# The softmax over a sequence's pages, traced in four parts between the next sequence's page steps

## The chip, the cores and the metric

The kernel runs on one core of a Trainium2 chip. It is one inference step of a one-layer hybrid decoder: a prompt of 1024 tokens and a sample group of 8 sequences, each with one new token and 4096 past ones. The metric is the device time of one execution in microseconds (us). The core has five engines that work side by side, each through its own instructions in order: TensorE (PE) for matrix products, VectorE (DVE), ScalarE (ACT), GpSimd (POOL), and SyncE (SP), which here mostly starts DMA transfers.

## The reference

One projection of the normalised input feeds three groups of heads: differential attention, a Mamba-2 SSD scan and a gated delta rule (GDN). Their outputs are joined, projected and added to the input. For the change only the attention of the sample group matters. Its keys and values lie in pages of 128 tokens, 32 for each sequence, found by a page table:

```python
k_past = cache_k[l, page_table].reshape(bs, past, H_A, 2 * DH_A)
v_past = cache_v[l, page_table].reshape(bs, past, H_A, DV_A)
...
logits = jnp.einsum('bqhmd,bkhmd->bmhqk', q, k).astype(jnp.float32) * (DH_A ** -0.5)
logits = logits + rel_pos_bias(q_pos, k_pos, table)
...
p = jax.nn.softmax(logits, axis=-1)
wts = p[:, 0] - lam * p[:, 1]
return jnp.einsum('bhqk,bkhd->bqhd', wts.astype(v.dtype), v)
```

There are 4 heads with two maps each, so 8 softmaxes for each sequence, over its 4096 past keys and its own new one; the weights are the first map's less lambda times the second's.

## The kernel before, in words

**Streams.** The work is written as Python generators. Each does a piece of work and then yields a number, the amount of it. `drive()` (L280) always advances the generator whose done share of its total is least, so the yielded numbers set how the pieces are interleaved in the program. The order in the program is in its turn the priority by which a scheduler orders each engine's instructions. The projection stream (`proj_fm`, L424, matmuls in L458) is the longest; it fills TensorE between 107 and about 870 us, beside the GDN stream (on VectorE the steps of a triangular solve, tile `U`, through the helper in L159) and the sample stream. In the last stretch the prompt's attention (scores L718 and L719, values L745), the rest of GDN, the SSD scan (L1268 to L1329), the single-token steps and the rest of the sample stream are interleaved.

**The sample stream** (`sample_attention`, L903) takes the sequences one after the other. For sequence b there are 16 page steps (`k_pages`, L835): SyncE starts the transfers of two pages of keys (L823), GpSimd multiplies them by the query (L840), and VectorE sums the products (L841) into the scores `lg`. Between the page steps of sequence b the values of sequence b - 1 are used: `v_load` (L883) takes one of three buffers `vt`, of two pages each, and `v_mul` (L889) multiplies two such buffers, four pages, with the weights `wz` into the one PSUM bank `pv` (L896). A `v_mul` is eight instructions on TensorE, and its first waits for all four pages. Below, such four pages are a group, numbered 0 to 7 in each sequence; sequences are numbered from 0.

**The softmax** (`page_softmax`, L843) follows when all pages of keys of b have been summed: the largest score on each partition (VectorE, `smx`), a transposition on TensorE (L851), the largest over the partitions and a diagonal matrix (VectorE, `sm` and `sdg`), a product that gives it to all partitions (L856), the subtraction (VectorE, after the copy `spm`), the exponential (ScalarE, `lg` and `ses`), sums (VectorE, `ssm`), a product that adds them over the partitions (L868), and on VectorE the division and the weights `wz` and `wself`. GpSimd clears the columns of `wz` that the sequence before used (L875). In the program all of this is one piece that yields 4.0.

SyncE also starts the loads and stores of other streams, in the same queue as the pages: the stores of the attention's output (`oA` to `mixd`, L531) and of the scan's (`yv` to `mixd`, L1329), and loads of Y (L1268), of GDN states (`gs`) and of the output projection's weights (`wo`, L1552).

Of the kernel before, what the change touches and what calls it, by code (L numbers as in the profile page):

```python
# [23 lines left out]
NS = 8  # L24
# [54 lines left out]
def bl(ap, n):  # L79
    return ap.unsqueeze(len(ap.shape)).broadcast_to(list(ap.shape) + [n])  # L80


def bm(ap, n):
    return ap.unsqueeze(1).broadcast_to([ap.shape[0], n] + list(ap.shape[1:]))
# [3 lines left out]
def trunk_kernel(  # L88
# [43 lines left out]
    def nm(s):  # L132
        uid[0] += 1
        return f"{s}_{uid[0]}"
# [4 lines left out]
    def half(shape=(P, 512), dt=F32, n="h"):  # L139
        return hp.tile(list(shape), dt, tag="h", name=nm(n))  # L140
# [4 lines left out]
    def bank(ring=None):  # L145

        r = ring or rings[-1]
        return PS[r].tile([P, 512], F32, tag="b", name=nm("b"))

    def small(shape, n, dt=F32, bufs=2):  # L150
        return sp.tile(shape, dt, tag=n, name=nm(n), bufs=bufs)

    def act(out, in_, func, bias=0.0, scale=1.0, accum=None):
        if accum is None:
            return S.activation(out, in_, func, bias=bias, scale=scale)  # L155
        return S.activation(out, in_, func, bias=bias, scale=scale, accum_out=accum)  # L156

    def tt(out, a, b, op):
        return V.tensor_tensor(out=out, in0=a, in1=b, op=op)  # L159
# [675 lines left out]
    def k_pages(b, qb, lg, g):  # L835
        kt = kvp.tile([P, 2, 512], F32, tag="kt", name=nm("kt"), bufs=KB)
        for j in range(2):
            page(cache_k, b * NPG + 2 * g + j, kt[:, j, :])
        with behind_gdn():
            G.tensor_tensor(out=kt, in0=kt, in1=bm(qb, 2), op=ALU.mult)  # L840
            V.tensor_reduce(out=lg[:, 2 * g:2 * g + 2, :], in_=kt.rearrange("p j (a d) -> p j a d", d=64), axis=AX.X, op=ALU.add)  # L841

    def page_softmax(b, lg):  # L843
        l31 = lg[:, NPG - 1, :].rearrange("p (h m) -> p h m", m=2)
        tt(l31, l31, bl(fb, 2), ALU.add)
        mx = small([P, 8], "smx")
        V.tensor_reduce(out=mx, in_=lg.rearrange("p g a -> p a g"), axis=AX.X, op=ALU.max)
        tt(mx, mx, slfb[:, b, :], ALU.max)

        pt = bank()  # L850
        TE.transpose(pt[0:8, 0:P], mx, ident)  # L851
        m8 = small([8, 1], "sm8")
        V.tensor_reduce(out=m8, in_=pt[0:8, 0:P], axis=AX.X, op=ALU.max)
        dg = small([8, 8], "sdg")
        V.tensor_scalar_mul(dg, ident[0:8, 0:8], m8)
        TE.matmul(pt[:, 256:264], ones[0:8, :], dg, start=True, stop=True)  # L856
        pmx = small([P, 8], "spm")
        V.tensor_copy(pmx, pt[:, 256:264])
        tt(lg, lg, bm(pmx, NPG), ALU.subtract)
        act(lg, lg, AF.Exp)  # L860
        es = small([P, 8], "ses")
        tt(es, slfb[:, b, :], pmx, ALU.subtract)
        act(es, es, AF.Exp)
        sm = small([P, 8], "ssm")
        V.tensor_reduce(out=sm, in_=lg.rearrange("p g a -> p a g"), axis=AX.X, op=ALU.add)
        tot = small([P, 8], "sto")
        pt = bank()
        TE.matmul(pt[:, 0:8], ones, sm, start=True, stop=True)  # L868
        tt(tot, pt[:, 0:8], es, ALU.add)
        V.reciprocal(tot, tot)  # L870
        tt(tot, tot, lsg.rearrange("p h m -> p (h m)"), ALU.mult)
        tt(lg, lg, bm(tot, NPG), ALU.mult)
        l4 = lg.rearrange("p g (h m) -> p g h m", m=2)
        if b > 0:
            G.memset(wz[:, :, 4 * b - 4:4 * b], 0.0)  # L875
        tt(wz[:, :, 4 * b:4 * b + 4], l4[:, :, :, 0], l4[:, :, :, 1], ALU.add)
        tt(es, es, tot, ALU.mult)
        e2 = es.rearrange("p (h m) -> p h m", m=2)
        tt(wself[:, b, :], e2[:, :, 0], e2[:, :, 1], ALU.add)

    vq = []

    def v_load(b, g):  # L883
        vt = kvp.tile([P, 2, 512], F32, tag="vt", name=nm("vt"), bufs=VB)
        for j in range(2):
            page(cache_v, b * NPG + 2 * g + j, vt[:, j, :])
        vq.append((b, g, vt, pages[-2:]))
# [13 lines left out]
                mybir.DependencyClass.Sync, mybir.DependencyReason.DATA), reason="four pages at once")  # L901

    def sample_attention():  # L903
        for b in range(NS + 1):
            if b < NS:
                qb = half(n="qb")
                SP.dma_start(out=qb, in_=qd[b:b + 1, :].broadcast_to([P, 512]))
                lg = small([P, NPG, 8], "lg")
            vg = 0
            for g in range(NPG // 2):  # L910
                if b < NS:
                    k_pages(b, qb, lg, g)
                    yield 2.4
                if b > 0:
                    want = 16 if b == NS else max(0, g - 2) * 16 // 13 + 1
                    while vg < min(16, g + VB if b == NS else want + 1):
                        if len(vq) == VB:
                            v_mul()
                            yield 1.0
                        v_load(b - 1, vg)  # L920
                        vg += 1
                    while len(vq) > 1 and vg - len(vq) + 1 < want and g > 2:
                        v_mul()
                        yield 1.0
            while vq:
                v_mul()
                yield 1.0
            if b < NS:
                page_softmax(b, lg)
                yield 4.0  # L930
        wd = small([NS, NS, 4], "wd", bufs=1)
        tt(wd, wself[0:NS], bl(ident[0:NS, 0:NS], 4), ALU.mult)
        TE.matmul(pv[0:32, :], wd, vS, start=False, stop=True)
        hm = small([P, 4], "hm", bufs=1)
        V.tensor_reduce(out=hm, in_=ident.rearrange("p (a h) -> p h a", h=4), axis=AX.X, op=ALU.add)
        sb = small([P, NS], "sb", bufs=1)
        V.tensor_reduce(out=sb, in_=ident.rearrange("p (j b h) -> p b j h", b=NS, h=4), axis=AX.XY, op=ALU.add)
        pvs = half(n="pvs")
        tt(pvs.rearrange("p (h d) -> p h d", d=P), pv.rearrange("p (h d) -> p h d", d=P), bl(hm, P), ALU.mult)
        pst = bank()  # L940
        TE.matmul(pst[0:NS, :], sb, pvs, start=True, stop=True)
        oS = half([NS, 512], n="oS")
        S.copy(oS, pst[0:NS, :])
        finish_sample(oS, 0)
        yield 1.0
# [733 lines left out]

    sample_q()  # L1680
    smp = sample_attention()
    drive((chain(items(1), small_cols()), 52.0), (take(smp, 16 * 2.4 - 0.1), 40.0))
    sample_k()
# [251 lines left out]
```

## Time and profile before

| | |
|---|---|
| time, median of 3 runs | 1310.28 us (1307.37 to 1313.32) |
| profiled execution | 1304.49 us |
| its span from first to last instruction | 1302.8 us |
| TensorE busy, matmuls | 1156.6 us, 89% |
| VectorE busy | 855.5 us, 66% |
| GpSimd busy | 585.1 us, 45% |
| ScalarE busy | 464.0 us, 36% |
| data moved by DMA | 275.56 MB, 212 GB/s in the mean |

The span is what the rows of the trace cover; the execution's own time is some 2 us longer. A row of the trace that names a wait (in square brackets, behind "idle before") tells how long the engine stood idle just ahead of the instruction and what then released it. An engine that is busy for less than the whole span need not be a limit, and its idle time costs nothing unless something that the end depends on is behind it.

### The profile page before, as it was taken

The page shows a single profiled execution, that of the slowest core. Times are in us where ns is not written, and L with a number is a line of the kernel's source. Part 1 is how long each engine was busy: PE and PEld are TensorE (multiplying, and loading weights), DVE is VectorE, ACT ScalarE, POOL GpSimd, SP SyncE. Part 2 cuts the span into 40 slices and gives each one's busy share as a digit, 9 for nine tenths or more (in the row PEclk, how much of TensorE's full clock was granted, in tenths as well). Part 3 has the DMA queues.
Part 4 walks back from the last instruction along what each step waited for, and adds up shares of the span by engine and source line. Part 5 has one row for each costly group of instructions (what it writes and reads, how often), then busy time and mean ns, then how long its engine had stood idle before and what let it go on. Part 6 is the DMA issues. An engine that isn't in the chain of part 4 may idle for free.

```text
span 1302.8 us, 22109 instructions
## 1 busy us (share of the span) xinstructions
PE 1156.6 (89%) x7445; PEld 970.2 (74%) x7445; DVE 855.5 (66%) x1994; ACT 464.0 (36%) x991; POOL 585.1 (45%) x395
## 2 busy tenths in 40 slices
PE   4999999979899989888987997878788899799997
PEld 3889897857688778768867786765566778688876
DVE  6624495398477769557449725878759879674444
ACT  6332232212223312324522242334527658552111
POOL 3757873463545653556546655633012232151100
PEclk9999998989899889999889998979889989899999
DMA  8656864985876953985876889799587373871410
GB/s 294 192 183 213 286 208 154 301 285 170 290 237 213 305 177 113 287 278 167 292 222 211 254 282 270 229 286 257 143 243 198 103 182 109 293 237 49 145 67 34
DMA packets 246450, 275.56 MB, mean 212 GB/s; under 512 B 31905, under 2 KB 163376, under 8 KB 246322
## 3 DMA queue, kind: packets, MB, share of 16 engines
q1 hardware_dynamic: 168082, 214.44, 52.1%
q10 hardware_dynamic: 78256, 59.72, 16.1%
q8 instruction: 59, 0.97, 0.3%
q14 instruction: 53, 0.43, 0.1%
HBM read 231.59 MB, written 42.67 MB: 211 GB/s over the span
## 4 chain that ended last, share of the span: by engine, by line
PE 44%; DMA 22%; DVE 19%; issue 4%; SPq 4%; POOL 3%; ACT 3%; ACTq 1%; POOLq 0%; DVEq 0%
PE b L458 16%; PE b L1824 9%; DMA kt<-in_cache_k_dram 4%; DMA vt<-in_cache_v_dram 4%; DVE U L159 4%; PE pv L896 4%; DVE lg L841 3%; DVE cy L167 2%; POOL kt L840 2%; DMA ql<-qfd 1%; DMA w<-in_w_in_dram 1%; SPq L823 1%; PE b L745 1%; DMA sbc<-bcd 1%; PE b L1051 1%
## 5 line engine op out<-in xcount | busy, mean ns | idle before, releaser
L458 PE MATMUL b<-hh,whi 128*128 128x344 f32 (+1 forms) x2016 | 505.2, 333 | 5.9 <-ACT whi L155 2.4
L840 POOL TENSOR_TENSOR kt<-kt,qb 128x1024 f32<-128x1024 f32 x128 | 307.0, 2403 | 228.0 <-DMA kt<-in_cache_k_dram 160.2
L458 PEld LDWEIGHTS b<-hh,whi 128*128 128x128 f32 x2016 | 358.9, 194 | 39.0 <-issue 28.1
L458 PE MATMUL b<-hh,wlo 128*128 128x344 f32 (+1 forms) x1008 | 330.2, 332 | 3.1 <-POOL wlo L201 2.9
L841 DVE TENSOR_REDUCE lg<-kt 128x16 f32<-128x1024 f32 x128 | 155.2, 1214 | 133.4 <-POOL kt L840 126.3
L458 PEld LDWEIGHTS b<-hh,wlo 128*128 128x128 f32 x1008 | 195.1, 194 | 20.8 <-issue 16.5
L201 POOL TENSOR_TENSOR wlo<-w,whi 128x512 fp32r<-128x512 f32 x86 | 111.6, 1302 | 99.9 <-ACT whi L155 87.2
L1824 PE MATMUL b<-wo,mh 128*128 128x512 f32 (+1 forms) x408 | 122.0, 381 | 0.3 <-POOL wo L1558 0.3
L896 PE MATMUL pv<-vt,wz 128*32 128x512 f32 x512 | 82.6, 671 | 23.5 <-DMA vt<-in_cache_v_dram 16.0
L155 ACT ACTIVATE whi<-w 128x512 fp32r<-128x512 f32 x86 | 53.9, 629 | 134.4 <-PE b L458 89.1
L167 DVE SCALAR_TENSOR_TENSOR cy<-b,vec,cy 128x341 f32<-128x341 f32 (+4 forms) x180 | 99.7, 566 | 1.6
L1824 PEld LDWEIGHTS b<-wo,mh 128*128 128x128 f32 x408 | 75.0, 189 | 14.9 <-POOL wo L1558 0.5
L1824 PE MATMUL b<-wo,ml 128*128 128x512 f32 (+1 forms) x204 | 77.2, 379 | 0.0
L1792 POOL TENSOR_TENSOR ml<-zt,mh 128x512 fp32r<-128x512 f32 x16 | 22.5, 1406 | 106.3 <-ACT mh L1791 101.3
L159 DVE TENSOR_TENSOR U<-U,Dm 128x60 f32<-128x60 f32 (+24 forms) x124 | 51.4, 415 | 24.9 <-DMA Dm<-invd 23.1
L156 ACT ACTIVATE e<-e,nmx 128x128 f32<-128x128 f32 (+7 forms) x64 | 49.0, 768 | 13.2 <-DVE nmx L723 7.0
L155 ACT ACT_TABLE_LOAD x30 | 38.5, 1283 | 40.0 <-DMA w<-in_w_in_dram 15.8
L718 PE MATMUL b<-kTh,qh 128*128 128x128 f32 (+3 forms) x96 | 41.8, 437 | 8.8 <-DVE mx L721 8.5
L159 DVE TENSOR_TENSOR y<-b,gate 128x512 f32<-128x512 f32 (+1 forms) x17 | 11.1, 660 | 52.4 <-PE b L1824 52.4
L159 DVE TENSOR_TENSOR U<-U 128x60 f32<-128x60 f32 (+24 forms) x124 | 44.0, 355 | 1.8
L969 DVE TENSOR_SCALAR cy<-b,vec 128x344 f32<-128x344 f32 (+1 forms) x60 | 33.4, 565 | 15.9 <-PE b L458 15.8
L1824 PEld LDWEIGHTS b<-wo,ml 128*128 128x128 f32 x204 | 38.4, 188 | 7.1
(528 smaller groups left out, 2032.3 us busy)
## 6 DMA issues: line engine op xcount, KB each, us to landing
kt<-in_cache_k_dram SPq DMA_DIRECT2D x256, 256.0 KB
vt<-in_cache_v_dram SPq DMA_DIRECT2D x256, 256.0 KB
w<-in_w_in_dram ACTq DMA_DIRECT2D x82, 256.0 KB
zfd<-zf ACTq DMA_DIRECT2D x12, 512.0 KB
wo<-in_w_out_dram SPq DMA_DIRECT2D x12, 512.0 KB
om<-mixd SPq DMA_DIRECT2D x24, 256.0 KB
xt<-in_x_prompt_dram SPq DMA_DIRECT2D x8, 512.0 KB
hx<-in_w_ada_dram SPq DMA_DIRECT2D x16, 256.0 KB
```

The costliest lines, as they stand in the source:

```text
L155: return S.activation(out, in_, func, bias=bias, scale=scale)
L156: return S.activation(out, in_, func, bias=bias, scale=scale, accum_out=accum)
L159: return V.tensor_tensor(out=out, in0=a, in1=b, op=op)
L167: return V.scalar_tensor_tensor(out=out, in0=a, scalar=s, in1=b, op0=op0, op1=op1)
L201: G.tensor_tensor(out=lo, in0=w32, in1=hi.bitcast(F32), op=ALU.subtract)
L458: TE.matmul(ps[:, 0:N], a, b[k][:, sl], start=(i == 0), stop=(i == 23))
L718: TE.matmul(ps[:, 0:b - a], qh[:, m, ts], kT[m][:, a:b], start=True, stop=False)
L840: G.tensor_tensor(out=kt, in0=kt, in1=bm(qb, 2), op=ALU.mult)
L841: V.tensor_reduce(out=lg[:, 2 * g:2 * g + 2, :], in_=kt.rearrange("p j (a d) -> p j a d", d=64), axis=AX.X, op=ALU.add)
L896: mm = TE.matmul(pv[32 * r:32 * r + 32, :], wz[:, 2 * g + j, :], vt[:, j, :], start=(b == 0 and g < 2), stop=(b == NS - 1 and g >= 14 and ...
L969: V.tensor_scalar_mul(y[:, c0_:c0_ + m], ps[:, o:o + m], wv[3])
L1824: TE.matmul(ps[c], m[a][:, kt % 4, :], w[kt][:, c[0]:c[1]], start=(kt == KT[0] and i == 0), stop=(kt == KT[-1] and i == 2))
```

## The change

`page_softmax` becomes a generator with four parts. The first ends after the largest score on each partition, the second after the diagonal matrix, the third after the sums, and the fourth is the rest. The second product (L856, 859 after) takes a PSUM bank of its own instead of the transposition's. In `sample_attention` only the first part is traced right behind a sequence's page steps; the other three come one at a time behind the first three page steps of the next sequence, each with a yield of 1.3. For the last sequence, which has no next one, they come one after the other ahead of the page loop, each with a yield of 4.0.

```diff
@@ page_softmax
         V.tensor_reduce(out=mx, in_=lg.rearrange("p g a -> p a g"), axis=AX.X, op=ALU.max)
         tt(mx, mx, slfb[:, b, :], ALU.max)
+        yield
 
         pt = bank()
         TE.transpose(pt[0:8, 0:P], mx, ident)
...
         V.tensor_scalar_mul(dg, ident[0:8, 0:8], m8)
+        yield
+        pt = bank()
         TE.matmul(pt[:, 256:264], ones[0:8, :], dg, start=True, stop=True)
...
         tot = small([P, 8], "sto")
+        yield
         pt = bank()
         TE.matmul(pt[:, 0:8], ones, sm, start=True, stop=True)
...
         tt(wself[:, b, :], e2[:, :, 0], e2[:, :, 1], ALU.add)
+        yield
@@ sample_attention
     def sample_attention():
+        soft = None
         for b in range(NS + 1):
...
             vg = 0
+            if b == NS:
+                for _ in soft:
+                    yield 4.0
             for g in range(NPG // 2):
                 if b < NS:
                     k_pages(b, qb, lg, g)
                     yield 2.4
+                if soft is not None and next(soft, 0) is None:
+                    yield 1.3
                 if b > 0:
...
             if b < NS:
-                page_softmax(b, lg)
-                yield 4.0
+                soft = page_softmax(b, lg)
+                next(soft)
```

Lines below the softmax have other numbers after: the products L896 are L901, and the scan's L1268 and L1329 are L1279 and L1340. The engines run the same instructions in another order. Three places show it. The first is TensorE's order at the end of sequence 4's values, before; `vt` is a buffer of two pages, `b` a PSUM bank of the projection, `hh` and `wlo` or `whi` its operands.

```order
L458 MATMUL b_7353<-hh_773,wlo_7088 128x344
L896 MATMUL pv<-vt_7283,wz 32x512 x2
L896 MATMUL pv<-vt_7343,wz 32x512 x2
L896 MATMUL pv<-vt_7383,wz 32x512 x2
L896 MATMUL pv<-vt_7460,wz 32x512 x2
L458 MATMUL b_7425<-hh_514,whi_7253 128x344
```

And after, at the same place:

```order
L901 MATMUL pv<-vt_7230,wz 32x512 x2
L901 MATMUL pv<-vt_7318,wz 32x512 x2
L458 MATMUL b_7438<-hh_514,whi_7277 128x344
L458 MATMUL b_7438<-hh_515,whi_7277 128x344
...
L458 MATMUL b_7572<-hh_515,whi_7277 128x344
L901 MATMUL pv<-vt_7356,wz 32x512 x2
L901 MATMUL pv<-vt_7422,wz 32x512 x2
```

Group 7 followed group 6 with nothing between; now 50 matmuls of the projection stand between the two.

The second place is TensorE's order at the end of the last sequence's values, sequence 7, after; `kTh` and `qh` are operands of the prompt's scores.

```order
L901 MATMUL pv<-vt_10907,wz 32x512 x2
L901 MATMUL pv<-vt_10919,wz 32x512 x2
L718 MATMUL b_11455<-kTh_10514,qh_11218 128x512
L719 MATMUL b_11455<-kTh_10514,ql_11219 128x512
L718 MATMUL b_11461<-kTh_10517,qh_11218 128x256
L719 MATMUL b_11461<-kTh_10517,ql_11219 128x256
L901 MATMUL pv<-vt_10966,wz 32x512 x2
L901 MATMUL pv<-vt_10978,wz 32x512 x2
L944 MATMUL pv<-vS,wd_11061 32x512
```

Four matmuls stand between groups 6 and 7 here. Before, the same two groups had 46 rows between them, among them these, which led up to the last group:

```order
L745 MATMUL b_10391<-vh_9746,wT_10367 128x128
L1291 LDWEIGHTS identb
L1291 MATMUL b_10783<-masks,identb 128x512
L1293 MATMUL b_10783<-nsels,rts 128x512
L1296 MATMUL b_10783<-rts,sels 128x128 x4
L1492 MATMUL b_10434<-gs_11122,gwz_11124 32x128 x8
L745 MATMUL b_10503<-vh_9746,wT_10452 128x128 x2
L896 MATMUL pv<-vt_10761,wz 32x512 x2
L896 MATMUL pv<-vt_10773,wz 32x512 x2
L933 MATMUL pv<-vS,wd_10808 32x512
```

The other streams' rows that stood there now stand elsewhere.

The third place is SyncE's queue among the last sequence's pages of values, after; an ISA row ahead of a page computes its address.

```order
L823 DMA vt_10721<-in_cache_v_dram 128x512
L531 DMA mixd<-oA_9481 128x8x128
L1340 DMA mixd<-yv_10066 128x512
L823 ISA
L823 DMA vt_10733<-in_cache_v_dram 128x512
L823 ISA
L823 DMA vt_10733<-in_cache_v_dram 128x512
L814 TENSOR_LOAD pt_1086
L823 ISA
L823 DMA vt_10749<-in_cache_v_dram 128x512
```

Before, the first store of `oA` stood behind the last page:

```order
L823 DMA vt_10773<-in_cache_v_dram 128x512
L1520 DMA gs_11566<-in_state_gdn_dram 128x8x128
L1520 DMA gs_11718<-in_state_gdn_dram 128x8x128
L531 DMA mixd<-oA_9444 128x8x128
L1329 DMA mixd<-yv_10068 128x512
```

So two stores of other streams now stand ahead of pages of sequence 7 that stood ahead of them.

## Rows read from the trace of the kernel before

**Rows 1.** The page: busy time of the engines; shares of the chain that ended last.

```profile
PE 1156.6 (89%) x7445; PEld 970.2 (74%) x7445; DVE 855.5 (66%) x1994; ACT 464.0 (36%) x991; POOL 585.1 (45%) x395
PE 44%; DMA 22%; DVE 19%; issue 4%; SPq 4%; POOL 3%; ACT 3%; ACTq 1%; POOLq 0%; DVEq 0%
```

**Rows 2.** TensorE's waits: line, releaser: us in total, times, longest us.

```profile
PE pv L896 <- DMA vt<-in_cache_v_dram: 16.0, 10, 4.6
PE b L851 <- DVE smx L159: 12.3, 4, 9.0
...
PE b L868 <- DVE ssm L865: 8.5, 3, 4.3
...
PE b L868 <- DVE U L159: 6.5, 1, 6.5
...
PE pv L896 <- DVE wz L159: 4.2, 3, 2.0
...
PE pv L896 <- DMA kt<-in_cache_k_dram: 2.8, 1, 2.8
```

**Rows 3.** TensorE's timeline, 452 to 464: start, us, line, tiles, count, [idle before].

```profile
453.17 1.06 PE L896 MATMUL pv<-vt,wz 128*32 128x512 f32 x8 [0.89 <-DMA vt<-in_cache_v_dram]
...
460.64 1.94 PE L896 MATMUL pv<-vt,wz 128*32 128x512 f32 x8 [4.56 <-DMA vt<-in_cache_v_dram]
```

**Rows 4.** TensorE's timeline, 673 to 683.

```profile
673.38 0.48 PE L458 MATMUL b<-hh,whi 128*128 128x344 f32 x2
673.70 0.32 PE L458 MATMUL b<-hh,wlo 128*128 128x344 f32 x1
673.95 1.06 PE L896 MATMUL pv<-vt,wz 128*32 128x512 f32 x8
679.39 1.94 PE L896 MATMUL pv<-vt,wz 128*32 128x512 f32 x8 [4.37 <-DMA vt<-in_cache_v_dram]
...
682.28 0.78 PE L458 MATMUL b<-hh,whi 128*128 128x344 f32 x2
```

**Rows 5.** TensorE's timeline, in 345 to 365 and in 638 to 641.

```profile
349.97 1.21 PE L896 MATMUL pv<-vt,wz 128*32 128x512 f32 x8 [2.84 <-DMA kt<-in_cache_k_dram]
...
639.38 1.07 PE L896 MATMUL pv<-vt,wz 128*32 128x512 f32 x8 [1.50 <-DMA vt<-in_cache_v_dram]
```

**Rows 6.** TensorE's timeline, 898 to 990.

```profile
949.71 1.94 PE L896 MATMUL pv<-vt,wz 128*32 128x512 f32 x8 [0.62 <-DMA vt<-in_cache_v_dram]
...
955.57 1.06 PE L896 MATMUL pv<-vt,wz 128*32 128x512 f32 x8 [0.41 <-DMA vt<-in_cache_v_dram]
956.56 0.50 PE L718 MATMUL b<-kTh,qh 128*128 128x512 f32 x1
956.90 0.39 PE L719 MATMUL b<-kTh,ql 128*128 128x512 f32 x1
```

**Rows 7.** TensorE's timeline, 857 to 868.

```profile
858.48 1.07 PE L896 MATMUL pv<-vt,wz 128*32 128x512 f32 x8
...
865.75 1.57 PE L896 MATMUL pv<-vt,wz 128*32 128x512 f32 x8
```

**Rows 8.** Timeline of all engines, 279 to 291.5.

```profile
282.61 2.34 POOL L840 TENSOR_TENSOR kt<-kt,qb 128x1024 f32<-128x1024 f32 x1
282.78 2.26 DVE L159 TENSOR_TENSOR U<-U,Dm 128x68 f32<-128x68 f32 x1
...
290.67 0.37 PE L851 MATMUL b<-ident,smx 128*8 128x128 f32 x1 [9.02 <-DVE smx L159]
```

**Rows 9.** A window: width; busy us of PE, PEld, DVE, ACT, POOL.

```profile
925.00:950.00 25.00, 18.40 (x115) 12.43 (x119) 21.91 (x117) 14.28 (x43) 1.04 (x1) 0.77 0.54 165
```

**Rows 10.** Instructions of the tile `ses`: durations in ns, min/median/max.

```profile
L159 DVE TENSOR_TENSOR ses<-slfb,spm x8: 153/160/2357, 195.4 to 918.2; 128x8 f32<-128x8 f32 x8
```

**Rows 11.** SyncE's waits: line, releaser: us in total, times, longest us.

```profile
SPq L531 <- DVE oA L159: 23.5, 4, 12.3
SPq L1268 <- PE b L1314: 16.9, 5, 8.3
```

## Prediction, made before the changed kernel was run

> **What bounds the kernel now.** I read the page's busy line and the shares of its chain first. TensorE is busy for 1156.6 of 1302.8 us, VectorE 855.5, GpSimd 585.1; the chain that ended last is TensorE for 44%, DMA 22%, VectorE 19% [rows 1]. TensorE works in order, so the span is its work plus its waits, and a change that removes no arithmetic can only move the waits. Then the list of TensorE's waits [rows 2], for what the softmax and the page products touch. The products `pv` wait for pages of V 16.0 us in 10 places, and 2.8 us in one that is put down to a page of K. The softmax makes it wait at the transposition L851 (12.3 us in 4, the longest 9.0), at the sum L868 (8.5 us in 3, the longest 4.3, and one of 6.5 behind a step of U), and at the first product of a sequence for `wz` (4.2 in 3). These add to 50.3 us, 4% of the span: the whole field of this change.
>
> Then the timelines about the longest of them. One `pv` row is eight instructions, four pages, and waits for all four. Three buffers of two pages are turned over, so two pages of a group can be fetched only when the group ahead is done. In [rows 3] a group starts at 453.17, lasts 1.06, and the next starts at 460.64 after a wait of 4.56: 6.4 us from an end to the next start is what two late pages take. In [rows 4] it is 675.01 to 679.39, 4.4 us, with nothing at all between. Before the wait one matmul of the projection takes 0.32 us and two take 0.48, so each further one costs 0.16; just behind it two take 0.78: the granted clock has fallen towards its lower level. So 6.4 us holds 40 such matmuls, and two groups that are closer stand still for the rest.
>
> **The change part by part.** No instruction's arithmetic goes or comes, and one bank more is taken for each softmax; the parts and their `yield`s are no instructions. The sum goes against the profiled execution, 1304.5 us, 5.8 below the median of the runs, 1310.3.
>
> *Waits for pages that go.* The softmax's weight in the interleaving is now spread over three steps, and so the groups of `pv` stand elsewhere among the projection's matmuls. In TensorE's order of before, the distance of a group from the one ahead, its own four rows counted, is 4 to 22 rows in seven places, and 37 to 54 after: sequence 1's group 4 (22 to 41), sequence 2's groups 6 and 7 (20 to 41, 12 to 47), sequence 4's groups 3 and 7 (14 to 37, 4 to 54), sequence 7's groups 3 and 4 (13 to 43, 15 to 39). Their waits: 2.84 [rows 5], 0.89 and 4.56 [rows 3], 4.37 [rows 4], 0.62 and 0.41 [rows 6]; and 1.50 for sequence 4's group 3 [rows 5]. Sum -15.2. The 3.6 us that are left of the 18.8 stand at places whose distances hardly change.
>
> *Waits for pages that come.* Other pairs move together. Sequence 6's groups 4 and 5 go from 40 and 29 rows to 24 and 25. In [rows 7] the 25 rows between its groups 4 and 5 of before were 29 less the group's own four; they took from 859.55 to 865.75, 6.2 us, 0.25 each. The 20 and 21 rows that stay are then 5.0 and 5.2 us: short by 1.4 and 1.2. Sequence 7's group 6 goes from 28 to 22 rows: 18 at 0.25 is 4.5, short by 1.9. Its group 7 goes from 50 to 8: four score matmuls remain, the like of which start 0.2 to 0.3 us apart [rows 6], so 1.0 us of 6.4 is covered, short by 5.4. Sequence 1's group 6 goes from 37 to 10 rows, but TensorE's few rows there stand in the delta rule's chain, which waits for VectorE and ScalarE of itself; I take 0.5, near the end of nothing, for the group ahead waited there too [rows 5] (0 to 5.4 are the ends). Sum +10.4 (5, where only the last pair isn't hidden, to 15).
>
> *The softmax's own waits.* The longest transposition wait, 9.02 us [rows 8], is that of sequence 1. It stays: TensorE's order has this transposition at the same place as before, since only page steps, which put nothing on TensorE, were put ahead of it. At the sum L868: sequence 7's 4.29 goes, since 88 instead of 19 matmuls now stand between L856 and L868 (-4.3; nothing if VectorE, busy for 21.9 of 25 us there [rows 9], is late with whatever takes its place). Sequence 5's wait of 6.5 behind U [rows 2] has 16 matmuls more ahead (2.6 us) and two VectorE rows more (0.43 us each, 855.5 over 1994): -1.7. Sequence 6's 1.7, part of the 8.5, has three matmuls more and seven VectorE rows more: +2.5. At the first product of the next stage, waiting for `wz`, the matmuls between L868 and it go from 71, 59, 55, 37, 37 to 45, 39, 46, 38, 31 for sequences 1 to 5, with VectorE rows 24, 20, 27, 14, 22 to 22, 19, 22, 15, 23. Three of these are the waits of [rows 2] (4.2 us), those of sequences 3 to 5; sequences 1 and 2 had none and lose 26 and 20 matmuls of their slack, which no row gives. By 0.16 and 0.43 us a row I take -0.7, +0.3 and +1.4 for the three, and, between nothing and the 4.2 and 3.2 us of those matmuls, +1.0 and +1.4 for the first two. All together about 0 (-6 to +10).
>
> *Cost at nothing.* The further bank: its first use is in the ring of banks that the softmax already drew from twice, and the transposition's bank is now free earlier; no wait of [rows 2] is for a bank of these. The clear of `wz` on GpSimd for sequence 7 now stands behind the last multiply of keys, so that multiply no longer waits with it; VectorE, not that multiply, is late there.
>
> *A rule weighed.* The softmax's steps of VectorE now stand among the page multiplies of GpSimd. What the trace shows: a step of U beside a multiply of 2.34 us took 2.26 [rows 8], and the small subtraction `ses`, 160 ns in the median, took 2357 ns once [rows 10]. The Trainium skill, "SBUF — State Buffer", section "Who interferes with whom", says that a VectorE instruction with two SBUF inputs and a GpSimd instruction that reads SBUF exclude each other for a whole instruction; these rows agree. By that rule every two-input step of parts two to four risks a multiply's length. By the rows the risk is not new: multiplies ran on both sides of the softmax already, and the extreme of 2357 is from before the change. I put nothing into the sum, and a rival below.
>
> The sum: 1304.5 - 15.2 + 10.4 + 0 = 1299.7 for a profiled execution, and with 5.8 more 1305 as a median.
>
> **The rivals.** Bound of telling: 0.5%, 6.5 us; within it a measurement of this kernel can't tell a change.
>
> *Waits go and nothing takes their place.* If the new close pairs are hidden (TensorE waits for something else between them, as the 0.25 us a row of [rows 7], more than the 0.16 of the projection alone, says that it did) and VectorE keeps up, it is -15.2 - 4.3 - 1.7, some -21, with the clock's recovery behind each wait (0.15 us for each of a few matmuls) on top; half of the new pairs hidden gives -15. Time 1289 to 1300, the middle 1295. For it: the seven places were much too close before, and the new ones mostly nearly fit. Against it: the last pair with 8 rows can't be hidden by its neighbours.
>
> *The last V pages stand behind a store.* The slower side. SyncE issues in order. Before, the store of head 0's output (L531) stood behind the last page of sequence 7. In the new order of SyncE the stores of the attention output (L531) and of `yv`, and a load of Y (L1268, 1279 after), stand between pages of sequence 7. SyncE's waits there are up to 12.3 and 8.3 us [rows 11]; both would hold pages back by up to 20.6 us, and a `pv` that lacks a page holds all that is behind it on TensorE. Less the 6.4 that one group's turn-over covers, that is 14: 1305 + 14 = 1319. It decides when TensorE reaches a group of sequence 7 before its store's data are there. Against it: the products of this sequence were moved back by some 40 to 180 rows too, and so more of the head's work is done by then.
>
> *Stretched softmax.* If the two two-input steps between L856 and L868 are each caught by a multiply, a softmax is later by twice the 2.2 us of [rows 10]; for seven, half of it uncovered, 15 us: 1320. For it: nothing keeps the multiplies away. Against it: the two steps had multiplies beside them before.
>
> *The change does next to nothing*, because its parts mostly keep their place on TensorE, as the 9.02 us wait does: 1308 to 1312. It falls into the forecast's own band.
>
> **How the numbers follow.** The forecast's case with the last rival beside it, within 0.5% of 1310.3: 0.40. Waits go: 0.38, faster. The store: 0.17, stretched softmax: 0.05, both slower. The forecast is 1305, near the edge of "faster", since a sum of terms of both signs gave -5; all its bounds at one end or the other (-15.2 with +5 and -6, or with +15 and +10) are 1294 and 1320, and half-way to each, its own range, 1300 to 1312. The whole range reaches from 1287 (all waits gone, and the clock) to 1324 (the store's price in full).
>
> **What would show it.** In the changed profile: the wait of `pv` for pages in the list falls from 18.8 to about 14 us, with the longest single one in sequence 7's last group, about 5; the 9 us transposition wait is still there; at L868 it waits about 4.8 and 4.3 us for sequences 5 and 6, and not for 7. It is wrong if `pv` waits in sequence 7 are above 10 us, if SyncE's L531 row has a page of V next to it, or if waits not named here (L718, L1216, L1291) grow by more than the sum.

## The result, and the profile after

The changed kernel is slower: 1323.77 us in the median of 8 runs (1316.21 to 1329.48), beside 1311.6 us for the kernel before (8 runs, 1305.91 to 1313.96). The ratio is 1.0096, with a 95% interval of 1.0068 to 1.0124; the forecast was 1305 us and "within 0.5%". The ratios here and below leave disturbed runs out, so they can differ a little from the quotient of two medians.

The profiled execution of the changed kernel has a span of 1323.9 us, 21.1 more than the one before; it is among the slower ones, so its sizes are larger than the median's 12. First the page: busy times of the engines, as in [rows 1], and the granted clock in 40 slices.

```profile
PE 1174.1 (89%) x7442; PEld 981.8 (74%) x7445; DVE 872.0 (66%) x1994; ACT 472.1 (36%) x996; POOL 584.8 (44%) x395
...
PEclk9999999989999999988888999967798899899999
```

TensorE does the same instructions and is busy 17.5 us longer. It runs longer at the lower clock: the slices with 6 and 7 are those between 860 and 960 us. The mean granted clock over all runs says the same: 0.9346 (8 runs), and 0.9394 for the kernel before (118 runs, from all comparisons). A run's time multiplied by its mean clock is roughly what it would take at full clock: 1236.4 us (standard error 1.7) after and 1229.3 (0.5) before. So of the 14 us between the two means some 7 are waiting and 7 are the lower clock; this is an estimate, since it lets waits shrink with the clock too. In the profiled pair the clock's part is larger: of the 21.1 us, 17.5 are longer busy time of TensorE and 3.6 more idle time.

Where is the time lost? The projection's last matmul (L458) starts at 860.8 us before and 862.0 after; the output projection's first starts at 1142.1 and 1163.2. Nearly all 21 us lie between the two, in the last stretch. There the table by windows says what happened; the columns are as in [rows 9], and the last three are granted clock, DMA share and GB/s. Before:

```profile
860.00:890.00 30.00, 21.92 (x120) 15.85 (x119) 24.92 (x79) 16.89 (x38) 10.52 (x6) 0.72 1.02 292
...
930.00:960.00 30.00, 25.71 (x149) 16.08 (x147) 23.27 (x126) 13.65 (x39) 1.73 (x4) 0.81 0.69 205
960.00:1000.00 40.00, 36.42 (x268) 28.70 (x267) 26.96 (x65) 20.35 (x61) 14.14 (x19) 1.00 0.84 229
1000.00:1040.00 40.00, 34.53 (x320) 29.61 (x318) 33.32 (x101) 28.55 (x79) 7.28 (x5) 1.00 0.44 120
```

And after:

```profile
860.00:890.00 30.00, 16.07 (x75) 10.04 (x75) 23.19 (x65) 11.04 (x25) 10.96 (x6) 0.60 0.97 250
...
930.00:960.00 30.00, 24.20 (x127) 19.85 (x128) 23.55 (x124) 20.59 (x63) 1.96 (x4) 0.73 0.20 63
960.00:1000.00 40.00, 38.06 (x253) 30.20 (x251) 32.59 (x98) 17.73 (x52) 15.03 (x19) 0.88 0.96 249
1000.00:1040.00 40.00, 33.40 (x270) 21.04 (x267) 19.87 (x72) 23.25 (x66) 3.79 (x3) 0.89 0.63 184
```

Three things are to be seen. Just behind the projection's end TensorE does 75 matmuls where it did 120. From 930 to 960 the DMA share is 0.20 where it was 0.69: the loads of V stand still, since their buffers are full and the products that would empty them can't run; the next load leaves at 967.2 us, just behind the first of these products. And from 960 on, where the clock was at its full level before, it is 0.88 and 0.89.

The reason for the second is the last softmax. Its chain before, on VectorE and TensorE (start, us, line, tiles; `smx` to L851, `sdg` to L856, `ssm` to L868):

```profile
912.46 0.42 PE L851 MATMUL b<-ident,smx 128*8 128x128 f32 x1
915.01 0.21 DVE L855 TENSOR_SCALAR sdg<-ident,sm 8x8 f32<-8x8 f32 x1
916.12 0.38 PE L856 MATMUL b<-sdg,ones 8*128 8x8 f32 x2
927.07 0.60 DVE L865 TENSOR_REDUCE ssm<-lg 128x8 f32<-128x256 f32 x1
927.73 0.59 PE L868 MATMUL b<-ssm,ones 128*128 128x8 f32 x2 [4.29 <-DVE ssm L865]
```

After:

```profile
918.44 0.41 PE L852 MATMUL b<-ident,smx 128*8 128x128 f32 x1
919.20 0.22 DVE L856 TENSOR_SCALAR sdg<-ident,sm 8x8 f32<-8x8 f32 x1
933.37 0.57 PE L859 MATMUL b<-sdg,ones 8*128 8x8 f32 x2
937.60 0.64 DVE L868 TENSOR_REDUCE ssm<-lg 128x8 f32<-128x256 f32 x1
959.88 0.43 PE L872 MATMUL b<-ssm,ones 128*128 128x8 f32 x2
```

The chain takes 41 us from the first row's start to the last one's, not 15, and no row of it waits: `sdg` is ready at 919.4 and its product runs at 933.4, `ssm` is ready at 938.2 and its product runs at 959.9, each behind matmuls of other streams that now stand ahead of it. The 4.29 us wait at the sum is gone as predicted. But the first products of sequence 7 start at 966.1 instead of 932.1 us, and the last ends at 1031.1 instead of 980.9.

Now the list of TensorE's waits, columns as in [rows 2].

```profile
PE b L852 <- DVE smx L159: 18.3, 3, 9.0
PE pv L901 <- DMA vt<-in_cache_v_dram: 15.1, 9, 3.6
PE pv L901 <- issue: 10.3, 4, 4.7
...
PE pv L901 <- DVE wz L159: 5.1, 3, 2.8
...
PE b L1073 <- ACT cy L155: 4.9, 1, 4.9
...
PE b L872 <- DVE ssm L868: 2.9, 1, 2.9
```

The waits for pages did not fall from 18.8 to 14 us. They are 25.4, if those that the trace puts down to "issue" are counted. Two of these are the longest, each behind a page whose load was started late. The one at sequence 4's group 7, 4.51 us, is where 4.37 was to go [rows 4]: 50 matmuls stand between the groups now, but loads of a state (`sst`, `sbc`) and what they wait for stand on SyncE between the group's pages. The other is at the projection's end. SyncE's timeline there:

```profile
858.53 0.33 SPq L823 DMA_DIRECT2D vt<-in_cache_v_dram  x1
862.91 0.38 SPq L531 DMA_DIRECT2D mixd<-oC  x1
863.48 0.44 SPq L823 DMA_DIRECT2D vt<-in_cache_v_dram  x1
```

And TensorE's:

```profile
867.27 1.94 PE L901 MATMUL pv<-vt,wz 128*32 128x512 f32 x8 [4.73 <-issue]
870.05 1.09 PE L1073 MATMUL b<-ident,cy 128*128 128x128 f32 x4 [0.85 <-DVE tail L987]
...
876.21 1.97 PE L1073 MATMUL b<-ident,cy 128*128 128x128 f32 x8 [4.86 <-ACT cy L155]
```

The store of the delta rule's head 2 (`oC`, L531) stands between the two pages of one buffer. SyncE stands at it until 862.91, the second page leaves at 863.48, and group 4 of sequence 6 waits for it. This is the rival of the store, at another store and another sequence than foretold. In the kernel before that store leaves at 874.02, between the pages of a later buffer.

### The profile page after: what moved, and what is told of

It is laid out like the page before. It is cut to its first block, busy times and chain, and to the rows that moved or that the text cites. A ratio compares the mean times of both kernels' runs of the same rounds, so it can differ in the third digit from the quotient of the medians.

```text
span 1323.9 us, 22100 instructions
## 1 busy us (share of the span) xinstructions
PE 1174.1 (89%) x7442; PEld 981.8 (74%) x7445; DVE 872.0 (66%) x1994; ACT 472.1 (36%) x996; POOL 584.8 (44%) x395
## 5 line engine op out<-in xcount | busy, mean ns | idle before, releaser
L458 PE MATMUL b<-hh,whi 128*128 128x344 f32 (+1 forms) x2016 | 507.6, 333 | 12.8 <-DVE cy L167 5.7
L458 PEld LDWEIGHTS b<-hh,whi 128*128 128x128 f32 x2016 | 362.0, 196 | 42.0 <-issue 35.0
L458 PE MATMUL b<-hh,wlo 128*128 128x344 f32 (+1 forms) x1008 | 333.1, 334 | 0.7 <-POOL wlo L201 0.7
L458 PEld LDWEIGHTS b<-hh,wlo 128*128 128x128 f32 x1008 | 196.5, 196 | 17.3 <-issue 15.7
L901 PE MATMUL pv<-vt,wz 128*32 128x512 f32 x512 | 85.3, 664 | 30.9 <-DMA vt<-in_cache_v_dram 15.1
L159 DVE TENSOR_TENSOR U<-U,Dm 128x60 f32<-128x60 f32 (+24 forms) x124 | 55.8, 450 | 13.1 <-DMA w<-in_w_in_dram 5.8
L159 DVE TENSOR_TENSOR U<-U 128x60 f32<-128x60 f32 (+24 forms) x124 | 54.0, 436 | 1.8
L745 PE MATMUL b<-vh,wT 128*128 128x128 f32 x288 | 43.3, 299 | 3.4 <-ACT oA L155 1.9
L901 PEld LDWEIGHTS pv<-vt,wz 128*32 128x32 f32 x512 | 12.3, 111 | 44.9 <-issue 24.8
```

Of the source, the lines that this page charges most:

```text
L458: TE.matmul(ps[:, 0:N], a, b[k][:, sl], start=(i == 0), stop=(i == 23))
L745: TE.matmul(po[:, 0:P], wTs[j // 4][:, j % 4, :], vh[:, j, :], start=(j == 0), stop=(j == i))
L901: mm = TE.matmul(pv[32 * r:32 * r + 32, :], wz[:, 2 * g + j, :], vt[:, j, :], start=(b == 0 and g < 2), stop=(b == NS - 1 and g >= 14 and ...
```

## The experiments

18 kernels were run, in five groups, each beside runs of the kernel before on the same chip. "Rows" are rows of TensorE's order behind the projection's end, equal neighbours counted as one; the last column is the row of the product that closes `pv`. The table gathers what was measured; the clock is a kernel's mean.

| run | median us (runs) | ratio to before (95%) | clock | last sum at row | products end at row |
|---|---|---|---|---|---|
| before | 1308.6, mean (118) | 1 | 0.9394 | 130 | 229 |
| changed | 1323.8 (8) | 1.0096 (1.0068 to 1.0124) | 0.9346 | 178 | 330 |
| e1_last_whole | 1318.9 (11) | 1.0046 (1.0006 to 1.0086) | 0.9355 | 108 | 206 |
| e2_only_last | 1310.8 (11) | 0.9991 (0.9948 to 1.0034) | 0.9360 | 194 | 359 |
| e3_last_yield | 1305.4 (11) | 0.9949 (0.9919 to 0.9980) | 0.9432 | 123 | 211 |
| e5_one_bank | 1326.4 (5) | 1.0123 (1.0068 to 1.0179) | 0.9310 | 180 | 334 |
| f1_store_later | 1322.9 (6) | 1.0103 (1.0057 to 1.0148) | 0.9372 | 166 | 328 |
| f2_store_later_whole | 1312.6 (12) | 1.0011 (0.9975 to 1.0047) | 0.9389 | 108 | 201 |
| f3_store_later_light | 1302.0 (12) | 0.9933 (0.9908 to 0.9959) | 0.9468 | 123 | 217 |
| e6_only_last_light | 1331.9 (6) | 1.0174 (1.0120 to 1.0229) | 0.9262 | 174 | 263 |
| g1_weight_067 | 1310.2 (11) | 1.0024 (0.9992 to 1.0057) | 0.9416 | 120 | 203 |
| g2_weight_267 | 1317.6 (7) | 1.0080 (1.0049 to 1.0111) | 0.9374 | 132 | 260 |
| g3_weight_8 | 1313.9 (11) | 1.0044 (1.0010 to 1.0077) | 0.9425 | 206 | 368 |
| g4_before_weight_12 | 1309.3 (11) | 0.9991 (0.9958 to 1.0024) | 0.9418 | 130 | 234 |
| k1_one_bank_last | 1307.1 (12) | 0.9962 (0.9929 to 0.9995) | 0.9430 | 121 | 228 |
| k2_one_bank_store_later | 1312.9 (12) | 1.0034 (1.0009 to 1.0058) | 0.9400 | 121 | 212 |
| k3_one_bank_all | 1322.6 (6) | 1.0104 (1.0069 to 1.0138) | 0.9327 | 130 | 250 |
| m1_only_last_one_bank | 1326.0 (6) | 1.0117 (1.0067 to 1.0168) | 0.9333 | 144 | 260 |
| p1_delta_first | 1323.7 (6) | 1.0115 (1.0075 to 1.0155) | 0.9350 | 179 | 312 |
| p2_before_delta_first | 1312.9 (12) | 1.0052 (1.0019 to 1.0085) | 0.9379 | 134 | 248 |

**Which part of the change.** The first group takes the change apart: the last softmax whole, the last one alone in parts, its parts lighter, and the bank.

```diff
# e1_last_whole
-            if b == NS:
-                for _ in soft:
-                    yield 4.0
...
                 next(soft)
+            if b == NS - 1:
+                for _ in soft:
+                    pass
+                yield 4.0
# e2_only_last
                 next(soft)
+            if b < NS - 1:
+                for _ in soft:
+                    pass
+                yield 4.0
# e3_last_yield
                 for _ in soft:
-                    yield 4.0
+                    yield 4.0 / 3
# e5_one_bank
         yield
-        pt = bank()
         TE.matmul(pt[:, 256:264], ones[0:8, :], dg, start=True, stop=True)
```

> As the changed kernel, but the softmax of the last sequence (7) is traced in one piece where it stood before, with one yield of 4.0; sequences 0 to 6 stay in four parts. Theory L (the loss of some 12 us is made by the last sequence, whose products now end at 1031 instead of 981 us in the profile, among the prompt's attention): 1308 to 1313 us, and the output projection starts near 1142 as before. Theory E (the splitting of sequences 0 to 6 shifts everything and the last stretch only shows it): still 1320 to 1326 us.

> Only the softmax of the last sequence is in four parts, with three yields of 4.0 ahead of its page loop; sequences 0 to 6 are whole as before. Theory L: 1320 to 1326 us. Theory E: 1308 to 1313 us. Both partly: between, near 1317.

> As the changed kernel, but the three parts of the last sequence yield 4.0/3 each, 4.0 in all as before, instead of 12.0. Theory L in the form that the amount of 12.0 puts the last sequence's products back (they end 20 rows ahead of the place of before in TensorE's order now): 1308 to 1314 us. If it is the cutting of the last softmax itself and not its weight: 1320 to 1326 us. Theory E: 1320 to 1326 us.

> As the changed kernel, but the second product of a softmax goes into the transposition's bank, as before. If the further bank costs something (a later bank for others): some us below 1323.8. If it is free, as predicted, and only the order's details change: 1320 to 1327 us.

Neither theory came through whole. The last softmax alone in parts costs nothing (0.9991), though its products end latest but one; so the last sequence alone is not the loss. The first seven in parts and the last whole cost about half of it (1.0046). And with all in parts and only the weight of the last one lowered from 12.0 to 4.0, the kernel is faster than the one before (0.9949). So in the changed kernel the loss needs the weight between the last softmax's parts: without it the loss is gone, and more. The bank taken away alone brings nothing (1.0123).

**The store in SyncE's queue.** A lower priority moves the store behind the pages.

```diff
-        ST.dma_start(out=mixd[0:T, col:col + P].rearrange("(t p) c -> p t c", p=P), in_=o)
+        with boost(-300):
+            ST.dma_start(out=mixd[0:T, col:col + P].rearrange("(t p) c -> p t c", p=P), in_=o)
```

> As the changed kernel, but the stores L531 have a lower priority, by 300 steps. In SyncE's queue this moves the store of the delta rule's head 2 (oC) from between the two pages of one buffer of V, the one that group 4 of sequence 6 waits for, to two buffers of V behind it; little else moves (the same edit on the kernel before moves nothing). Theory S (this store holds a page, TensorE waits 4.7 us for it just behind the projection's end, its clock falls, and the delta rule's next head is late): 1311 to 1316 us. Theory W (the loss is the products of sequence 7, moved into a stretch where TensorE is full): still 1321 to 1326 us.

> Sequence 7's softmax whole (as in the earlier run with the last softmax whole, 1318.9 us) and the store of head 2 moved behind by the lower priority. Theory S: 1308 to 1312 us, since the hold was all that this kernel had worse than the one before. Otherwise: 1317 to 1321 us.

> The last softmax in parts that yield 4.0/3 each (1305.4 us before) and the store of head 2 moved behind. Theory S: 1296 to 1301 us, faster than the kernel before by some 0.9%. If the hold costs nothing on its own (its idle time is taken back later): 1303 to 1307 us.

Behind the two kernels with an early last chain the gain is 0.35 and 0.16 points of ratio, both within the intervals; in the changed kernel it is nothing (1.0103 beside 1.0096). In k2 (below) the same edit goes with a loss. In f1 the 4.73 us wait is gone, and TensorE waits at the next place, 9.7 us in one, for VectorE's `tail` of the last projected column:

```profile
857.71 1.94 PE L902 MATMUL pv<-vt,wz 128*32 128x512 f32 x8 [0.57 <-issue]
869.30 1.09 PE L1074 MATMUL b<-ident,cy 128*128 128x128 f32 x4 [9.66 <-DVE tail L988]
```

The hold is real in the trace, but that it costs time at the end is not shown.

**The weight.** e6 completes the square of e2 and e3 (only the last softmax in parts, with the light weights), and three kernels vary the weight in the changed kernel. g4 gives the whole softmax of the kernel before the weight 12.0.

```diff
# e6_only_last_light: e2_only_last, and
                 for _ in soft:
-                    yield 4.0
+                    yield 4.0 / 3
# g1, g2, g3: the changed kernel with 0.67, 2.67 and 8.0 there
# g4_before_weight_12
                 page_softmax(b, lg)
-                yield 4.0
+                yield 4.0 if b < NS - 1 else 12.0
```

> Only the softmax of sequence 7 in parts, and each yields 4.0/3; sequences 0 to 6 whole. It fills the square with the kernel before, the changed one and the runs with the last sequence alone. If the weight of 12.0 alone costs (theory W): 1300 to 1308 us, below the 1310.8 of the same with 12.0. If the weight matters only where sequences 0 to 6 are split too: 1309 to 1313 us.

> As the changed kernel, but each part of sequence 7's softmax yields 0.67 instead of 4.0; the products of sequence 7 end 203 rows of TensorE behind the projection's end, instead of 330 (211 with 1.33, which took 1305.4 us). Theory W (the later these products run, the more they cost): 1303 to 1307 us. Theory C (what costs is close groups, and a softmax with nothing between its products, whenever it is): slower than with 1.33, like the whole softmax in this place, 1313 to 1319 us.

> The same with 2.67 each (8.0 in all, products end at 260 rows). Theory W: between 1305.4 (1.33) and 1323.8 (4.0), near 1313 us. Theory C: by the groups' distances (11, 7, 19, 16, 16, 23, 24 rows, none below 7) as fast as with 1.33, 1303 to 1308 us.

> The same with 8.0 each (24 in all, products end at 368 rows). Theory W: 1325 to 1332 us. Theory C: the groups are 18, 34, 16, 26, 18 and 14 rows apart, wider than with 4.0, so 1310 to 1320 us.

> The kernel before, with the whole softmax of sequence 7 yielding 12.0 instead of 4.0 behind it. Its order differs only at the last group of products, some five rows later. All theories: 1308 to 1314 us; a larger difference would say that a few rows in the last stretch are enough to move the time by what the change does.

The kernel e6 was expected to be fast or unchanged by either reading and is the slowest of all. Its trace shows the price of close groups at its plainest; three groups stand 2 rows apart:

```profile
993.47 1.93 PE L901 MATMUL pv<-vt,wz 128*32 128x512 f32 x8 [2.59 <-DMA vt<-in_cache_v_dram]
998.81 1.93 PE L901 MATMUL pv<-vt,wz 128*32 128x512 f32 x8 [3.40 <-DMA vt<-in_cache_v_dram]
1004.30 1.94 PE L901 MATMUL pv<-vt,wz 128*32 128x512 f32 x8 [3.56 <-DMA vt<-in_cache_v_dram]
```

With nothing between them a group waits 3.4 to 3.6 us for its pages, where I had put 6.4, and at the lower clock it takes 1.93 us. Yet by the estimate of the time at full clock e6 takes 1230.3 us (standard error 2.8), no more than the kernel before on its chip (1228.7): nearly all of its loss is the clock, 0.9262.

In the changed kernel the weights 0.67, 1.33, 2.67, 4.0, 8.0 give the ratios 1.0024, 0.9949, 1.0080, 1.0096, 1.0044. That is no straight line, and the theories fare no better: 0.67 lies between the ranges of the two, 2.67 well above theory C's and 8.0 well below theory W's. But the time at full clock (time by mean clock) rises nearly steadily, 1232.4, 1231.4, 1234.9, 1236.4, 1239.1 us (standard errors 1.3 to 2.7): in this series later products go with more waiting, and the clock adds or takes some 10 us on top by no rule that I found. Outside the series that doesn't hold: e2, whose products end at row 359, has the lowest time at full clock of all, 1224.4 us. The weight of 12.0 behind a whole softmax does nothing (0.9991): there the products hardly move.

**The ring of banks.** That last run says that the weight itself isn't what moves the products. In the last stretch the sample stream takes its PSUM banks from a ring of three that other streams share:

```python
RA, RT, RB, RS, RO = "ps", "pt", "pj", "pj", "pj"
PSB = {"pj": 3, "ps": 2, "pt": 1, "pd": 1}
RG = "pj"
```

RB, RS, RO and RG are the scan, the single tokens, the sample stream and the delta rule. Each part of the softmax takes a turn in that ring, and with 4.0 between two parts the other streams' turns come in between, in program order. k1 leaves weights and parts alone and takes the turns away: the three products of sequence 7's softmax use one bank.

```diff
         yield
-        pt = bank()
+        if b < NS - 1:
+            pt = bank()
         TE.matmul(pt[:, 256:264], ones[0:8, :], dg, start=True, stop=True)
...
-        pt = bank()
-        TE.matmul(pt[:, 0:8], ones, sm, start=True, stop=True)
-        tt(tot, pt[:, 0:8], es, ALU.add)
+        if b < NS - 1:
+            pt = bank()
+        TE.matmul(pt[:, 384:392], ones, sm, start=True, stop=True)
+        tt(tot, pt[:, 384:392], es, ALU.add)
```

> As the changed kernel, with the weights of 4.0, but the three products of sequence 7's softmax use one PSUM bank, taken once at its transposition, instead of three turns of the ring. In TensorE's order its sum then stands 121 rows behind the projection's end instead of 178, and the products of sequence 7 end at 228 instead of 330. Theory B (the ring's turns make the chain late, and late products cost): 1303 to 1308 us, as with a weight of 1.33. Theory W (the weight itself costs): 1320 to 1325 us.

> The same, with the store of the delta rule's head 2 moved behind by a lower priority. Theory B and a hold that costs 3 us where the chain isn't late: 1299 to 1304 us, the fastest with the one of 1302.0. If the hold's idle time is taken by the next wait anyway: 1303 to 1308 us.

> One bank for the three products in every sequence's softmax. The products of sequence 7 end at 250 rows. Theory B: 1304 to 1312 us, at least 10 us below the 1326.4 of the run in which the first two products share a bank and the third takes its turn. Theory W: 1320 to 1327 us.

k1 has all of the change but the turns, and is 16.7 us faster than the changed kernel (0.9962 and 1.0096, intervals far apart). Its chain in the trace:

```profile
925.61 0.27 PE L852 MATMUL b<-ident,smx 128*8 128x128 f32 x1
...
926.24 0.22 DVE L856 TENSOR_SCALAR sdg<-ident,sm 8x8 f32<-8x8 f32 x1
...
928.10 0.38 PE L860 MATMUL b<-sdg,ones 8*128 8x8 f32 x2
...
929.80 0.61 DVE L869 TENSOR_REDUCE ssm<-lg 128x8 f32<-128x256 f32 x1
...
930.90 0.28 PE L874 MATMUL b<-ssm,ones 128*128 128x8 f32 x2
```

It takes 5 us instead of 41, with the weights of 4.0 still there. So in the changed kernel the weight acts through the ring's turns: together they make the last chain late, and with either of them taken away (e3, k1) the loss is gone. k2 and k3 show the limit of it. k2, with the store moved too, is slower than k1 (1.0034; 1299 to 1308 us were expected), and k3, with one bank in every softmax, has a short last chain and is as slow as the changed kernel.

**What is left.** m1 takes the turns out of e6; p1 and p2 give the delta rule's stream priority.

```diff
# m1_only_last_one_bank: e6_only_last_light with the diff of k1
# p1 (changed kernel), p2 (kernel before)
     OFF[sts[3][0]] = 2000
+    OFF[sts[1][0]] = 200
```

> Only sequence 7's softmax is in parts, with weights of 4.0/3, and its three products use one bank. The products of sequence 7 stand 157 to 258 rows behind the projection's end, 8 to 24 rows apart (190 to 261 and at the end 4, 2 and 2 apart, in the run of 1331.9 us without this). Theory C (late and close groups wait for their pages, some 3.5 us each, and the clock falls behind): 1306 to 1313 us. If how late the products end is what costs: still 1325 to 1332 us, since they end at the same row.

> As the changed kernel, and the delta rule's stream has priority by 200 steps in the last stretch. In TensorE's order its last solve (L1167) stands 12 rows earlier, the products of sequence 7 end at 312 rows instead of 330. Theory D (head 3's solve and the 16 steps behind it set the end of the last stretch; the late chain of the softmax costs only what it delays them): 1308 to 1315 us. If that is only a sign of other delays: 1319 to 1325 us.

> The kernel before with the same priority; its solve moves by four rows only, the products of sequence 7 end 19 rows later. Theory D: 1306 to 1312 us. A difference above 6 us to the kernel before would say that any shift in the last stretch moves the time by as much.

m1's groups end at the same row as e6's (260 and 263) without being close, and it stays slow (1326.0): close groups aren't what makes e6 slow either. p1 has head 3's solve earlier and stays slow (1323.7): that theory falls. p2 moves a few rows of the kernel before and costs 0.5%. So the time of the last stretch answers to its order in ways that none of the five readings (late products, close groups, the held page, the ring, the delta rule's head 3) covers for all kernels.

A sixth reading, of what the late products hold up, covers more of them. The scan works in eight blocks, and each begins on TensorE with transpositions of its Y (L1273 before, L1284 after). The product with `pvs` (L941 before, L952 after) closes the sample stream, needs the last product of `pv`, and takes a turn of the ring of three. In the changed kernel the scan's fourth block has the next turn and stands in TensorE's order one row behind it, at row 334; before it stood at row 315, behind the delta rule's solve. The trace before:

```profile
985.79 1.02 PE L941 MATMUL b<-pvs,sb 128*8 128x512 f32 x2 [1.85 <-DVE pvs L159]
...
1010.73 0.66 PE L1273 MATMUL b<-ident,Y 128*128 128x128 f32 x4
```

And after, with the step of VectorE that waits for the block, and GpSimd's steps about it:

```profile
1031.23 2.35 POOL L1569 TENSOR_TENSOR wo<-wo,wo 128x1024 fp32r<-128x1024 f32 x1 [30.83 <-PE pv L901]
...
1034.03 1.88 PE L952 MATMUL b<-pvs,sb 128*8 128x512 f32 x2
1035.84 0.73 PE L1284 MATMUL b<-ident,Y 128*128 128x128 f32 x4
...
1036.61 0.69 DVE L159 TENSOR_TENSOR xdt<-b,spl 128x512 f32<-128x512 f32 x1 [2.93 <-PE b L1284]
...
1037.38 1.04 POOL L1291 TENSOR_TENSOR xe<-xdt,dec 128x512 f32<-128x512 f32 x1 [3.80 <-DVE xdt L159]
```

The block starts 25 us later, and the output projection 21. (GpSimd stands 30.8 us too, for a buffer of V that `wo` takes over; but its next step then waits 3.8 us more for VectorE, so this isn't what holds the scan.) In five kernels, the changed one, e5, f1, k3 and p1, the turn of `pvs` is the one ahead of that block and the block begins at rows 319 to 336: all five are 1.0 to 1.2% slower. In k1 and k2 the turns follow each other so too, but `pvs` runs at rows 296 and 300. And e2 and g3, whose products end last of all, have the block ahead of them, at rows 299 and 286; in e2 it runs before `pvs`:

```profile
1003.95 0.66 PE L1288 MATMUL b<-ident,Y 128*128 128x128 f32 x4
...
1027.23 1.03 PE L956 MATMUL b<-pvs,sb 128*8 128x512 f32 x2
```

This order was read after the runs, and no run moves that turn alone, so it fits and is not shown. It leaves out g2, m1 and e6, slower by 0.8 to 1.7% with the block at row 316 or 317, behind the solve as before. What makes these slow stays open.

## Why the prediction was wrong

**The step that failed: sequence 7's chain was taken as free.** "Sequence 7's 4.29 goes, since 88 instead of 19 matmuls now stand between L856 and L868." They do, and it went. But these rows were not only cover for the chain, they were its delay: the chain is 26 us longer (41 instead of 15). The sum counts -4.3 for it and has no term for what hangs on its end. The products of sequence 7, "moved back by some 40 to 180 rows", were counted as a point against the slower rival; in the changed kernel they are part of the loss. Lighter weights (e3) or a chain without its turns (k1) give back 18.4 and 16.7 us.

**The cost at nothing.** "The further bank: its first use is in the ring of banks that the softmax already drew from twice ... no wait of [rows 2] is for a bank of these." For the one further bank this holds: e5 takes it away and is as slow. What it left out is the turns. I looked for a wait for a bank, and no row of the last chain waits for one after either. A ring's price is in the order: a turn that is taken later in program order stands behind every turn that other streams take before. The three turns of sequence 7's chain were 9 and 10 rows apart in TensorE's order, and are 22 and 52 apart, since any turn now comes behind 4.0 of other streams' work. k1 shows what that costs in this kernel, 16.7 us; that it is no fixed price, k3 shows.

**"A change that removes no arithmetic can only move the waits."** The prediction took TensorE's work as fixed and the 50.3 us of listed waits as the whole field. TensorE's busy time grew by 17.5 us, by the lower clock, and over all runs about half of the loss is clock. What brings the lower clock stays open.

**Pages.** Of the seven waits that were to go, five went (those of sequence 2, of sequence 4's group 3 and of sequence 7), one shrank (2.84 to 1.69), and 4.37 came back as 4.51. Of those that were to come, sequence 7's group 7 waits 1.94 and not 5.4, its group 6 0.47 and not 1.9, since other waits and a page's turn-over of 3.5 instead of 6.4 us take up the rest; sequence 6's group 4 waits 4.73 and not 1.4, for the store, and its group 5 1.48, near the 1.2 foretold. Three places for which nothing was forecast wait longer: sequence 3's groups 2 and 6 3.64 and 1.98, sequence 5's group 3 1.77. Up to the projection's end it comes to +1.2 us. The term of -15.2 with +10.4 was wrong in most places and, like its sum of -5, small beside what it left out.

**The other softmaxes.** Sequence 1's wait of 9.0 us stayed, as said. At the sum only sequence 5 still waits, 2.9 us and not 4.8; sequence 6, foretold at 4.3, does not. But sequence 5's wait did not shrink as a whole: 6.5 us at the sum became these two, at the transposition and the sum, 10.8 together.

```profile
709.13 0.37 PE L852 MATMUL b<-ident,smx 128*8 128x128 f32 x1 [7.89 <-DVE smx L159]
...
725.45 0.60 PE L872 MATMUL b<-ssm,ones 128*128 128x8 f32 x2 [2.92 <-DVE ssm L868]
```

**The rivals.** The slower one had the right place, the last stretch, and a mechanism that does occur, but not the one that decides: the store's hold could be taken away without a gain. The stretched softmax was not seen; VectorE's steps in the last chain take 0.2 to 0.6 us, and the longest `ses` of all eight is 2.37 us, where it was 2.36. For the part of the loss that is clock (0.9394 to 0.9346) I had no term on the slower side at all.

## What to carry to other kernels

When a chain is cut into pieces that are traced between other work, count its turns in every shared ring of buffers, not only its instructions: each turn goes behind all turns traced before it, and no wait in the profile of before shows that. Look, too, which stream has the next turn behind the one that gets late. Rows put between two links of a chain are cover for the link's wait and delay for what hangs on the chain's end; look which of the two is needed. And where several streams are interleaved up to a common end, an order changed by a few rows moves this kernel by up to 0.5% with no instruction more or less (p2), so a forecast needs a range of that size on both sides, and a first experiment that takes the cut back piece by piece; the best of the kernels here, 0.7% faster than before, was found that way (f3, light weights and the store later).

## What was not expected of the hardware

Kernels with the same arithmetic run at mean granted clocks from 0.9262 to 0.9468, and the share of time lost to the clock differs between them by up to 29 us (98.0 and 69.2 us, a run's time by one minus its clock), more than by any wait. In the changed kernel's trace the falls from 960 us on stand behind waits of only 1 to 2 us, as here, where a matmul group at the end takes 1.93 instead of 1.07 us:

```profile
1023.90 1.07 PE L901 MATMUL pv<-vt,wz 128*32 128x512 f32 x8 [0.47 <-issue]
...
1026.73 0.38 PE L718 MATMUL b<-kTh,qh 128*128 128x256 f32 x1 [1.10 <-DVE mx L721]
...
1029.17 1.93 PE L901 MATMUL pv<-vt,wz 128*32 128x512 f32 x8 [1.94 <-DMA vt<-in_cache_v_dram]
```

Which waits bring a fall and which don't could not be read from these traces, and the runs of one kernel differ by up to 2%.
